# Where the split activations of a two-block transformer kernel begin in SBUF

## The chip, the core and the metric

The kernel runs on one core of a Trainium2 chip. TensorE (PE) multiplies, VectorE (DVE) and ScalarE (ACT) do the element-wise work, GpSimd (POOL) does a few memsets, SyncE (SP) issues the transfers of the weights. The metric is the device time of one execution in microseconds; the time before is the median of three executions.

## What is computed

Two transformer blocks, one after the other, on one sequence of 256 tokens by 1024 features in float32. The first mixes stick-breaking attention with a recurrence (RWKV-7) and ends in a gated feed-forward; the second mixes dilated attention with a gated convolution, attends to a memory of 256 rows, and ends in a squared-ReLU feed-forward. Cut to the products with weights:

```python
# first block
proj = rms_norm(x) @ w_in                       # 1024 -> 5376
merged = gates0 * (o_sb @ w_sb_out) + gates1 * (o_rw @ w_rw_out)
x = x + rms_norm(merged @ w_o)
f = (silu(h @ w_ffn_gate) * (h @ w_ffn_up)) @ w_ffn_down   # 1024 -> 2816 -> 1024
x = x + rms_norm(f)
# second block
x = x + concat(rms_norm(attn), rms_norm(conv)) @ w_out     # from h @ w_in_2, 1024 -> 3072
x = x + softmax(q k^T / 16) v @ w_o_mem                    # q from h, k and v from mem
x = x + relu(h @ w_up)**2 @ w_down                         # 1024 -> 4096 -> 1024
return rms_norm(x)
```

## The kernel before

**How a product with weights is made.** Every float32 operand is split into a rounded high part and the rest: an activation `x` into `xh` and `xl`, a weight slab into `whi` and `wlo`. Three matmuls replace one: `xh·whi`, `xl·whi`, `xh·wlo`. Weights come in slabs of 512 KB (128 partitions of 4 KB each), a `wraw` buffer of three in turn; `slab` (L171) issues the transfer on SP's queue, casts to `whi` on ACT (L182) and subtracts to `wlo` on DVE (L183). A slab holds 4 row blocks of 256 columns, so it feeds 4 x 2 x 3 = **24 matmuls** in `block` (L247): for each half of the columns and each row block the three products above.

**Which operand moves.** In the usual case a 128 x 128 piece of `whi` or `wlo` is loaded into the array (the stationary operand, 512 bytes in each partition) and 256 columns of an activation, 1024 bytes in each partition, are streamed against it (the moving operand). In a name of the profile such as `mm<-xh,whi` the moving operand stands first. With `tok=True` (`w_sb` columns for v, the v columns of `w_in_2` and of `w_kv_mem_2`) the roles are swapped: `mm<-whi,xh`. The last product, `w_down_2` in `tokens`, is swapped too, with slabs of 512 columns: 512 columns of `whi` or `wlo` move against 128 tokens of `ah` or `al`, in 384 matmuls at L262.

**The activations.** `gh, gl` (unnormed input of the first three groups of `w_rw`), `xh, xl` (140 slabs: most of both blocks), `sh, sl` and `oh, ol` (outputs of attention and recurrence), `zh, zl` with the upper half of `xh, xl` (`w_o`), `fh, fl` (22 slabs' worth of `w_ffn_down`), `memh, meml` (8 slabs for k, 8 for v), `yh, yl` (`w_out_2`, 8 slabs), `xoh, xol` (`w_o_mem_2`, 8 slabs), `ah, al` (`w_down_2`).

**What sets the places in SBUF.** Tiles are laid out by pools that stack up in the order in which they are opened, each tile at the next multiple of 32 bytes. The pools of the weights, `wraw`, `whi`, `wlo`, begin at a multiple of 1024 in each partition, so a stationary piece of a slab begins 0 or 512 bytes behind a multiple of 1024. An activation begins where the tiles under it happen to end: `cst`, `vec` and small tiles of 8, 16 or 32 bytes among them. Each row block of an activation is 1024 bytes long, so all row blocks of one begin equally far behind a multiple of 1024.

## Time and profile before

| | |
|---|---|
| median of three executions | 851.95 us (851.76 to 854.29) |
| the profiled execution | 853.44 us, of which its span 851.7 us |
| granted TensorE clock, mean over the span | 0.994 of 2.4 GHz |
| PE busy | 829.5 us, 97% of the span, 6508 matmuls |
| DVE, ACT, POOL busy | 565.3, 464.9, 5.4 us |
| mean rate of the transfers | 168 GB/s, DMA engines busy 30 to 80% of each slice |

Matmuls overlap in the pipeline: a matmul of 256 columns is listed as 280 ns long, while the next one starts some 118 ns after it. How fast TensorE goes is therefore read from the distance between the starts of matmuls, not from their length.

### The profile page before, as it was taken

Reading aid. Unit: us, or ns where it says so; the run is one execution under the profiler, and the core shown is the slowest. Engines: PE = TensorE matmul, PEld = TensorE weight load, DVE = VectorE, ACT = ScalarE, POOL = GpSimd, SP = SyncE. Lnnn points to the kernel's source line nnn. Section 1 sums busy time; section 2 is a strip of 40 time slices with the busy share of each in tenths; the row PEclk is TensorE's granted clock in tenths of the full one; section 3 lists DMA queues with packets and bytes.
Section 4 is the critical chain, followed back from the end, with each engine's and each line's share of the span. In section 5 each row is a group of like instructions: output and inputs, shape, how many; then the busy total and the mean of one; then the engine's idle time right before and its main releaser. Section 6 shows DMA issues by size and latency. Waiting matters only on the chain.

```text
span 851.7 us, 15759 instructions
## 1 busy us (share of the span) xinstructions
PE 829.5 (97%) x6508; PEld 788.4 (93%) x6508; DVE 565.3 (66%) x790; ACT 464.9 (55%) x714; POOL 5.4 (1%) x14
## 2 busy tenths in 40 slices
PE   5999998999999999999999999999999999999996
PEld 5798987999999999999999998999999999988884
DVE  6858689455888776666545876689576666654543
ACT  6497355643577654445445657457455565553432
POOL 0001001000000000000000000000000000000000
PEclk9999999999999999999999999999999999999999
DMA  8434443542464765555555564455524555556551
GB/s 283 149 133 159 136 130 117 160 140 87 145 251 144 225 189 183 195 177 197 173 187 186 158 202 149 148 174 184 188 95 153 176 172 177 193 178 193 179 193 50
DMA packets 44631, 142.88 MB, mean 168 GB/s; under 512 B 8976, under 2 KB 9744, under 8 KB 44304
## 3 DMA queue, kind: packets, MB, share of 16 engines
q1 hardware_dynamic: 43840, 139.25, 50.7%
q10 hardware_dynamic: 720, 2.63, 0.8%
q8 instruction: 51, 0.84, 0.4%
q14 instruction: 20, 0.16, 0.1%
HBM read 139.17 MB, written 2.69 MB: 167 GB/s over the span
## 4 chain that ended last, share of the span: by engine, by line
PE 90%; DVE 5%; DMA 2%; ACT 2%; issue 1%; SPq 0%; ACTq 0%; DVEq 0%
PE mm L247 68%; PE mm L262 11%; DMA wraw<-in_w_rw 2%; PE pz L262 2%; DVE wlo L183 1%; PE po L262 1%; ACT whi L182 1%; PE px L262 1%; PE mgnh L262 1%; PE nv L262 1%; DVE prw L736 1%; PE kv L247 1%; PE ssum L262 1%; DVE pr L718 1%; DVE TF L719 0%
## 5 line engine op out<-in xcount | busy, mean ns | idle before, releaser
L183 DVE TENSOR_TENSOR wlo<-wraw,whi 128x1024 fp32r<-128x1024 f32 x254 | 308.2, 1215 | 198.8 <-ACT whi L182 197.3
L182 ACT CAST whi<-wraw 128x1024 fp32r<-128x1024 f32 x254 | 264.8, 1044 | 291.5 <-PE mm L247 174.9
L247 PE MATMUL mm<-xh,whi 128*128 128x256 f32 x1120 | 319.3, 285 | 0.0
L247 PE MATMUL mm<-xh,wlo 128*128 128x256 f32 x1120 | 316.1, 282 | 1.8 <-DVE wlo L183 1.8
L247 PE MATMUL mm<-xl,whi 128*128 128x256 f32 x1120 | 316.1, 282 | 0.0
L247 PEld LDWEIGHTS mm<-xh,whi 128*128 128x128 f32 x1120 | 212.0, 189 | 3.8 <-issue 2.2
L247 PEld LDWEIGHTS mm<-xh,wlo 128*128 128x128 f32 x1120 | 211.8, 189 | 2.9 <-DVE wlo L183 2.2
L247 PEld LDWEIGHTS mm<-xl,whi 128*128 128x128 f32 x1120 | 211.8, 189 | 0.9 <-issue 0.7
L262 PE MATMUL mm<-whi,ah 128*128 128x512 f32 x128 | 50.6, 395 | 0.0
L262 PE MATMUL mm<-whi,al 128*128 128x512 f32 x128 | 50.6, 395 | 0.0
L262 PE MATMUL mm<-wlo,ah 128*128 128x512 f32 x128 | 50.6, 395 | 0.0
L247 PE MATMUL mm<-fh,whi 128*128 128x256 f32 x176 | 49.1, 279 | 0.0
L247 PE MATMUL mm<-fl,whi 128*128 128x256 f32 x176 | 49.1, 279 | 0.0
L247 PE MATMUL mm<-fh,wlo 128*128 128x256 f32 x176 | 49.1, 279 | 0.0
L247 PEld LDWEIGHTS mm<-fl,whi 128*128 128x128 f32 x176 | 33.1, 188 | 0.0
L247 PEld LDWEIGHTS mm<-fh,wlo 128*128 128x128 f32 x176 | 33.1, 188 | 0.0
L247 PEld LDWEIGHTS mm<-fh,whi 128*128 128x128 f32 x176 | 33.1, 188 | 0.0
L262 PEld LDWEIGHTS mm<-whi,al 128*128 128x128 f32 x128 | 24.1, 188 | 5.8
L262 PEld LDWEIGHTS mm<-wlo,ah 128*128 128x128 f32 x128 | 24.1, 188 | 5.8
L262 PEld LDWEIGHTS mm<-whi,ah 128*128 128x128 f32 x128 | 24.1, 188 | 5.7
L247 PE MATMUL rw<-gh,whi 128*128 128x256 f32 x48 | 14.2, 296 | 9.0 <-ACT whi L182 9.0
L247 PE MATMUL mm<-memh,whi 128*128 128x256 f32 x64 | 18.8, 294 | 0.0
(349 smaller groups left out, 1379.9 us busy)
## 6 DMA issues: line engine op xcount, KB each, us to landing
wraw<-in_w_up SPq DMA_DIRECT2D x32, 512.0 KB, 3.5
wraw<-in_w_down SPq DMA_DIRECT2D x32, 512.0 KB, 4.3
wraw<-in_w_in SPq DMA_DIRECT2D x24, 512.0 KB, 4.2
wraw<-in_w_ffn_gate SPq DMA_DIRECT2D x22, 512.0 KB, 3.8
wraw<-in_w_ffn_up SPq DMA_DIRECT2D x22, 512.0 KB, 3.3
wraw<-in_w_ffn_down SPq DMA_DIRECT2D x20, 512.0 KB, 3.5
wraw<-in_w_gate SPq DMA_DIRECT2D x16, 512.0 KB, 3.3
wraw<-in_w_kv_mem SPq DMA_DIRECT2D x16, 512.0 KB, 3.3
```

The costliest lines, as they stand in the source:

```text
L182: nc.scalar.copy(hi[:, :w], raw[:, :w])
L183: nc.vector.tensor_sub(lo[:, :w], raw[:, :w], hi[:, :w].bitcast(F32))
L247: self.nc.tensor.matmul(ps[:, c, :], lhsT, rhs, start=first, stop=last, skip_group_check=True)
L262: self.nc.tensor.matmul(out, lhsT, rhs, start=start, stop=stop, skip_group_check=True)
L718: nc.vector.tensor_mul(pr[:, :, :, :t + 1], tri[:, :, :, :t + 1], q)
L736: nc.vector.tensor_mul(pr, left[:, r:r + 4, :].rearrange("p r (o i) -> p r o i", o=1).to_broadcast([P, 4, 16, 16]), right.rearrange("p (o ...
```

## The change

Tiles are created in another order, some small ones move into a new tile `small`, and tiles called `shift` are put in as fill. A `shift` tile has one instruction, a memset of one element in each partition on POOL. After it every split activation begins 192 bytes behind a multiple of 1024, and `ah, al` 832 bytes behind one. The weights' pools move too, but still begin at a multiple of 1024. `oh, ol` of the recurrence come from the ring of tag `s4` and no longer from that of tag `rv`. The small tiles `st`, `st2` and `rt` move to other pools.

Bytes behind a multiple of 1024 at which the operands begin, in the two built programs, and the same for the **distance** (begin of the moving operand minus begin of the stationary one, taken modulo 512, since the two halves of a slab's columns are 512 bytes apart):

| activation | before | after | distance before | distance after |
|---|---|---|---|---|
| `xh, xl`, `zh, zl` moving | 480 | 192 | 480 | 192 |
| `gh, gl` | 800 | 192 | 288 | 192 |
| `sh, sl` | 800 | 192 | 288 | 192 |
| `oh` / `ol` | 672 / 544 | 192 | 160 / 32 | 192 |
| `memh, meml` moving | 256 | 192 | 256 | 192 |
| `fh, fl` | 288 | 192 | 288 | 192 |
| `yh, yl` | 320 | 192 | 320 | 192 |
| `xoh, xol` | 352 | 192 | 352 | 192 |
| `xh, xl` stationary | 480, 992 | 192, 704 | 32 | 320 |
| `memh, meml` stationary | 256, 768 | 192, 704 | 256 | 320 |
| `ah, al` stationary | 320, 832 | 832, 320 | 192 | 192 |

(The token halves of a stationary activation lie 512 bytes apart, so there are two begins.)

The core of the diff:

```diff
+PHASE = 192
@@ class Net
         self.keep = pool("keep")
+        self.cst = self.keep.tile([P, NRES], F32, name="cst")
+        self.vec = self.keep.tile([P, NVEC], F32, name="vec")
+        self.small = self.keep.tile([P, 8], F32, name="small")
+        self.ones = self.keep.tile([P, P], F32, name="ones")
         self.pr = pool("wraw", 3)
         self.ph = pool("whi", 4)
         self.pl = pool("wlo", 4)
-        self.cst = self.keep.tile([P, NRES], F32, name="cst")
-        self.vec = self.keep.tile([P, NVEC], F32, name="vec")
-        self.xh = self.keep.tile([P, KC, T], F32R, name="xh")
...
+        acts = pool("acts")
+        self.shift(acts, PHASE)
+        self.xh = acts.tile([P, KC, T], F32R, name="xh")
+        self.xl = acts.tile([P, KC, T], F32R, name="xl")
+        self.zh = acts.tile([P, NP, T], F32R, name="zh")
+        self.zl = acts.tile([P, NP, T], F32R, name="zl")
+
+    def shift(self, pool, bytes_):
+        t = pool.tile([P, bytes_ // 4], F32, name="shift")
+        self.nc.gpsimd.memset(t[:, 0:1], 0.0)
@@ first
         one = ctx.enter_context(tc.tile_pool(name="one", bufs=1))
+        n.shift(one, 608)
         s4 = ctx.enter_context(tc.tile_pool(name="s4", bufs=14))
         dr = ctx.enter_context(tc.tile_pool(name="dr", bufs=1, space=DRAM))
+        n.shift(ctx.enter_context(tc.tile_pool(name="gap", bufs=1)), 640)
...
-            oh, ol = norm["o"] = [s4.tile([P, NP, T], F32R, tag="rv", name=k, bufs=3) for k in ("oh", "ol")]
+            oh, ol = norm["o"] = [s4.tile([P, NP, T], F32R, tag="s4", name=k) for k in ("oh", "ol")]
@@ memory
-    rt = n.rstd_tok(mem, [acc], D)
+    rt = n.rstd_tok(mem, [acc], D, out=n.small[:, 4:6])
@@ hybrid
         pool = ctx.enter_context(tc.tile_pool(name="hyb", bufs=1, reuse_waits="tile"))
+        yh = pool.tile([P, KC, T], F32R, name="yh")
+        yl = pool.tile([P, KC, T], F32R, name="yl")
...
-            st = tmp.tile([P, 2, 8], F32, tag="st2", name="st2", bufs=2)
+            st = pool.tile([P, 2, 8], F32, tag="st2", name="st2", bufs=2)
@@ cross
         pool = ctx.enter_context(tc.tile_pool(name="xat", bufs=1, reuse_waits="tile"))
+        oh = pool.tile([P, KC, T], F32R, name="xoh")
+        ol = pool.tile([P, KC, T], F32R, name="xol")
...
-            st = tmp.tile([P, 8], F32, tag="st", name="st", bufs=4)
+            st = pool.tile([P, 8], F32, tag="st", name="st", bufs=4)
@@ mlp
         pool = ctx.enter_context(tc.tile_pool(name="mlp", bufs=1, reuse_waits="tile"))
+        n.shift(pool, 832 - PHASE)
+        ah = pool.tile([P, 32, T], F32R, name="ah")
+        al = pool.tile([P, 32, T], F32R, name="al")
```

No engine but POOL gets, loses or reorders an instruction. POOL's row before, from the first memset of the recurrence (`TF` its block-diagonal factor, `SA` its states, `TT` its transposed inverse) to its end:

```order
L709 MEMSET TF 128x544 [waits DVE_49,Activation_49]
L713 MEMSET TF 64x8 [waits Pool_49]
L713 MEMSET TF 64x8 x3
L842 MEMSET SA_1849 128x1024 [waits DVE_49,Pool_49]
L842 MEMSET SA_1850 128x1024 [waits DVE_49,PE_49]
L842 MEMSET SA_1851 128x512 [waits DMAHW4_49,DMAHW3_49,DVE_49]
L751 MEMSET TT_1319 128x1024 [waits DMAHW6_49,DMAHW5_49,DMAHW7_49,DVE_49,Activation_49]
L751 MEMSET TT_1320 128x1024 [waits DMAHW1_49,DVE_49,PE_49]
```

Three memsets of `shift` now stand ahead of it and one behind it. And this is the same row after:

```order
L121 MEMSET shift 128x1 x3
L720 MEMSET TF 128x544 [waits DVE_49,Activation_49]
L724 MEMSET TF 64x8 [waits Pool_49]
L724 MEMSET TF 64x8 x3
L853 MEMSET SA_1861 128x1024 [waits DVE_49,Pool_49]
L853 MEMSET SA_1862 128x1024 [waits DVE_49,PE_49]
L853 MEMSET SA_1863 128x512 [waits DMAHW4_49,DMAHW3_49,DVE_49]
L762 MEMSET TT_1331 128x1024 [waits DMAHW6_49,DMAHW5_49,DMAHW7_49,DVE_49,Activation_49]
L762 MEMSET TT_1332 128x1024 [waits DMAHW1_49,DVE_49,PE_49]
L121 MEMSET shift 128x1 [waits DVE_49,PE_49]
```

The last `shift` waits for readers of the tiles that lay in its place. On ACT one cast of `oh`, at the end of the recurrence, has other waits. Before:

```order
L145 ACTIVATE lgv<-lgv 128x512 [waits Activation_49]
L266 CAST oh<-yc 128x512 [waits DVE_49]
L182 CAST whi<-wraw 128x1024 [waits DMAHW4_49,PE_49]
L266 CAST oh<-yc 128x512 [waits DVE_49]
L182 CAST whi<-wraw 128x1024 [waits DMAHW5_49,PE_49]
```

After, on the same engine and at the same place:

```order
L156 ACTIVATE lgv<-lgv 128x512 [waits Activation_49]
L277 CAST oh<-yc 128x512 [waits DMAHW4_49,DVE_49,Pool_49]
L193 CAST whi<-wraw 128x1024 [waits DMAHW4_49,PE_49]
L277 CAST oh<-yc 128x512 [waits DVE_49]
L193 CAST whi<-wraw 128x1024 [waits DMAHW5_49,PE_49]
```

`oh` lies where `TT` lay, so its first cast also waits for `TT`'s memset and transfer.

## Rows read from the trace of the kernel before

**Rows 1.** Busy us, share of the span and number of instructions, from the page.

```profile
PE 829.5 (97%) x6508; PEld 788.4 (93%) x6508; DVE 565.3 (66%) x790; ACT 464.9 (55%) x714; POOL 5.4 (1%) x14
```

**Rows 2.** Waits of PE: us in total, times, longest.

```profile
PE rw L247 <- ACT whi L182: 9.0, 1, 9.0
```

**Rows 3.** The chain that ended last: by line, then pieces (start us, us, what).

```profile
by line: PE mm L247 68.5%; PE mm L262 10.7%; DMA wraw<-in_w_rw 2.0%; PE pz L262 1.7%; DVE wlo L183 1.3%; PE po L262 0.9%; ACT whi L182 0.8%; PE px L262 0.8%; issue 0.8%; PE mgnh L262 0.7%; PE nv L262 0.7%; DVE prw L736 0.7%; PE kv L247 0.7%
...
16.06 5.93 DMA wraw<-in_w_rw
...
126.66 1.90 DVE prw L736
...
291.79 175.21 PE mm L247 x1488
```

**Rows 4.** Timeline of PE, `xh` moving: start us, us, what; rows 24 matmuls apart.

```profile
300.15 0.28 PE L247 MATMUL mm<-xh,whi 128*128 128x256 f32 x1
...
302.99 0.28 PE L247 MATMUL mm<-xh,whi 128*128 128x256 f32 x1
```

**Rows 5.** Timeline of PE, 24 apart: `sh` moving.

```profile
220.85 0.28 PE L247 MATMUL mm<-sl,whi 128*128 128x256 f32 x1
...
223.65 0.28 PE L247 MATMUL mm<-sl,whi 128*128 128x256 f32 x1
```

**Rows 6.** Timeline of PE, 24 apart: `xh` stationary, then `ah` stationary (512 columns).

```profile
505.22 0.28 PE L247 MATMUL mm<-whi,xh 128*128 128x256 f32 x1
...
508.03 0.28 PE L247 MATMUL mm<-whi,xh 128*128 128x256 f32 x1
...
800.05 0.40 PE L262 MATMUL mm<-wlo,ah 128*128 128x512 f32 x1
...
805.65 0.40 PE L262 MATMUL mm<-wlo,ah 128*128 128x512 f32 x1
```

**Rows 7.** Timeline of PE, 24 apart: `memh` moving, `memh` stationary, `xoh` moving.

```profile
264.57 0.28 PE L247 MATMUL mm<-meml,whi 128*128 128x256 f32 x1
...
267.45 0.28 PE L247 MATMUL mm<-meml,whi 128*128 128x256 f32 x1
...
274.91 0.28 PE L247 MATMUL mm<-whi,meml 128*128 128x256 f32 x1
...
277.79 0.28 PE L247 MATMUL mm<-whi,meml 128*128 128x256 f32 x1
...
646.43 0.28 PE L247 MATMUL mm<-xol,whi 128*128 128x256 f32 x1
...
649.31 0.28 PE L247 MATMUL mm<-xol,whi 128*128 128x256 f32 x1
```

**Rows 8.** Timeline of PE, 24 apart: `yh` moving, then `gh` moving.

```profile
578.89 0.28 PE L247 MATMUL mm<-yl,whi 128*128 128x256 f32 x1
...
581.72 0.28 PE L247 MATMUL mm<-yl,whi 128*128 128x256 f32 x1
...
17.93 0.28 PE L247 MATMUL rw<-gl,whi 128*128 128x256 f32 x1
...
20.76 0.28 PE L247 MATMUL rw<-gl,whi 128*128 128x256 f32 x1
```

**Rows 9.** PE by stretch (us): length, busy (matmuls), granted clock, DMA share, GB/s.

```profile
300.00:400.00 100.00, 100.00 (x847) 1.00 0.56 185
405.50:466.50 61.00, 61.00 (x526) 1.00 0.59 183
263.50:274.00 10.50, 10.50 (x90) 1.00 0.26 92
```

**Rows 10.** Timeline of POOL: its last memset, and what it waited for.

```profile
143.51 0.96 POOL L751 MEMSET TT<- 128x1024 f32 x1 [0.50 <-DMA wraw<-in_w_gate]
```

**Rows 11.** Costliest groups, from the page: busy us, mean ns, idle before, its releaser.

```profile
L183 DVE TENSOR_TENSOR wlo<-wraw,whi 128x1024 fp32r<-128x1024 f32 x254 | 308.2, 1215 | 198.8 <-ACT whi L182 197.3
L182 ACT CAST whi<-wraw 128x1024 fp32r<-128x1024 f32 x254 | 264.8, 1044 | 291.5 <-PE mm L247 174.9
```

More of the change, by code (lines that the diff above doesn't have):

```diff
@@ L104, in __init__ @@
         self.pl = pool("wlo", 4)
-        self.cst = self.keep.tile([P, NRES], F32, name="cst")
-        self.vec = self.keep.tile([P, NVEC], F32, name="vec")
-        self.xh = self.keep.tile([P, KC, T], F32R, name="xh")
-        self.xl = self.keep.tile([P, KC, T], F32R, name="xl")
-        self.zh = self.keep.tile([P, NP, T], F32R, name="zh")
-        self.zl = self.keep.tile([P, NP, T], F32R, name="zl")
+        acts = pool("acts")
[7 more added lines that the diff above has]
+        self.nc.gpsimd.memset(t[:, 0:1], 0.0)
     def psum(self, ctx, **bufs):
@@ L293, in rstd_sum, with rstd_tok @@
         return r
-    def rstd_tok(self, pool, parts, width, square=None):
+    def rstd_tok(self, pool, parts, width, square=None, out=None):
         pr = self.ax("rtok")
@@ L301, in rstd_tok @@
                         start=i == 0 and t == 0)
-        rt = pool.tile([P, 2], F32, name="rt")
+        rt = pool.tile([P, 2], F32, name="rt") if out is None else out
         self.act(rt, pr[:, 0:2], AF.Ln, bias=self.eps, scale=1.0 / width)
@@ L366, in network @@
     n = Net(ctx, tc, io)
-    keep = n.keep
-    eps = keep.tile([P, 4], F32, name="eps")
+    eps = n.small
     nc.vector.memset(eps[:, 0:1], EPS)
@@ L372, in network @@
     nc.vector.memset(eps[:, 3:4], 10.0 * math.log(2.0))
-    n.ones = keep.tile([P, P], F32, name="ones")
     nc.vector.memset(n.ones, 1.0)
@@ L1117, in hybrid @@
         ws, wts = {}, {}
-        yh = pool.tile([P, KC, T], F32R, name="yh")
-        yl = pool.tile([P, KC, T], F32R, name="yl")
         half = [slice(64 * r_, 64 * r_ + 64) for r_ in range(2)]
@@ L1213, in cross @@
         nc.vector.tensor_scalar(rn, rt, -1.0, None, op0=ALU.mult)
-        oh = pool.tile([P, KC, T], F32R, name="xoh")
-        ol = pool.tile([P, KC, T], F32R, name="xol")
         qh, ql, ws, wts = {}, {}, {}, {}
@@ L1320, in mlp @@
         banks = n.together([("w_up_2", g) for g in range(4)], n.xh, n.xl, norm)
-        ah = pool.tile([P, 32, T], F32R, name="ah")
-        al = pool.tile([P, 32, T], F32R, name="al")
         n.weave(turned())
```

## The prediction

> **What bounds the kernel now.** I read the busy times first: PE 97%, DVE 66%, ACT 55%, POOL 1% [rows 1]. As a busy PE is no proof of a bound, the waits of PE came next: the longest is 9.0 us, once, at the start, where the first slabs come in [rows 2]. The chain that ended last says the same: the products with weights (L247 and L262) are most of it; DMA and DVE stand on it only at the start and in the recurrence (the pieces at 16 and at 126 us), and from 291.79 us on one piece holds 1488 matmuls [rows 3]. So from about 211 us on the end is set by the distance between the starts of matmuls. Ahead of that PE is also full for long stretches, but DVE and ACT have a share of the chain.
>
> That distance is the thing to look at. Rows 24 matmuls (one slab) apart give it to half a nanosecond, as 0.01 us over 24 is 0.4 ns:
>
> - `xh` moving: 302.99 - 300.15 = 2.84 us, 118.3 ns each [rows 4]; over 100 us, (100 + 0.28)/847 = 118.4 [rows 9].
> - `sh` moving: 2.80 us, 116.7 ns [rows 5]; `fh` moving, over 61 us: 61.28/526 = 116.5 ns, 2.80 us too [rows 9].
> - `xh` stationary: 2.81 us, 117.1 ns; `ah` stationary, 512 columns: 5.60 us, 233.3 ns, which is 2 x 116.7 [rows 6].
> - `memh` moving, `memh` stationary, `xoh` moving: 2.88 us, 120.0 ns [rows 7].
> - `yh` and `gh` moving: 2.83 us, 117.9 ns [rows 8].
>
> The same instruction on the same shape, at the same granted clock of 1.00, the level of 2.4 GHz [rows 9], takes 116.7 to 120.0 ns. What differs is where the operands begin. By distance (moving minus stationary, modulo 512; the table of the change): 288 gives 2.80 and, with `gh`, 2.83; 320 gives 2.83; 480 gives 2.84; 256 and 352 give 2.88; 32 (`xh` stationary) gives 2.81; 192 (`ah`) gives 2.80 for each 256 columns. It is not the moving begin alone: with `xh` and with `memh` stationary the weights move from the same begins and take 2.81 and 2.88 [rows 6, 7]. It isn't the transfers either: the stretch with `memh` has the slower matmuls and half the traffic, 92 GB/s against 183 with `fh` [rows 9]. I call 2.80 us a slab the floor, because three distances and both lengths meet there and no row lies under it.
>
> **The change part by part.** No instruction of PE, DVE, ACT or SP is added, taken away or reordered; what is to be priced is the distance of 192.
>
> *The price of a slab at 192.* The one row with this distance is `ah`, at the floor, but its matmuls are twice as long [rows 6]. The nearest of 256 columns are `yh` at 320 and `gh` at 288, both 2.83, and `sh` and `fh` at 288, at 2.80 [rows 5, 8, 9]. Modulo 128 the slowest, 256 and 352, fall on 0 and 96, the fast ones on 32 and 64, and 192 falls on 64. Ends: 2.80 (nothing in the trace is lower; I allow a little below it for the range) and 2.88 [rows 7]. I take 2.80, by the row that has the distance itself.
>
> *The sum, in slabs of 24 matmuls, before minus after:*
>
> - `xh, xl` moving, 140 slabs: 140 x 0.04 = 5.6 us [rows 4, 5]. 768 of these 3360 matmuls, 32 slabs, start before 211 us, where DVE or a DMA is partly on the chain [rows 3]. I count half of their 1.28 us, so 5.6 - 0.64 = 4.96.
> - `zh, zl`, 4 slabs with the begin of `xh`: 0.16.
> - `memh` moving and `xoh` moving, 8 slabs each: 16 x 0.08 = 1.28 [rows 7].
> - `yh`, 8 slabs, 8 x 0.03 = 0.24, and `gh`, 6 slabs, 0.18 [rows 8].
> - `fh`, 22 slabs, `sh`, 4, and the 384 matmuls with `ah`: at the floor already, 0. `ah`'s two begins only trade places.
> - `memh` stationary, 8 slabs: its distance becomes 320, which is `yh`'s before, so 2.88 - 2.83: 0.40 [rows 7, 8]. `xh` stationary, 8 slabs, goes to 320 too: 2.81 to 2.83, a loss of 0.16 [rows 6, 8].
> - `oh`, 4 slabs with two begins in turn: left at 0; its ends are -0.16 and +0.32 by the rows above.
>
> 4.96 + 0.16 + 1.28 + 0.24 + 0.18 + 0.40 - 0.16 = **7.1 us**.
>
> *The rest at nothing.* The four memsets of one element stand on POOL, which is busy 5.4 us in all [rows 1]; three run at the start, and the last comes behind all other POOL work, where only the kernel's end stands behind it; the readers that it waits for are done in the memory attention. The first cast of `oh` now waits for the memset and the transfer of `TT`; the memset ends at 144.5 us [rows 10], and the recurrence multiplies with `TT` long before `oh` exists, so this wait has run out when ACT gets to it. If it had not, the casts of slabs queued behind it on ACT would be late, and PE with them. The products with two float32 operands (scores, recurrence) get other begins too, some better, some worse. By the chain's lines they are some 5% of it [rows 3]; I have no row that sorts them by begin and put them at 0, with half a microsecond either way in the range. DVE and ACT read and write at other begins; no row prices that. They wait for PE in the dense part, so a few ns on each would be covered.
>
> If TensorE runs 1.4% faster there, each slab is wanted in 2.80 us. DVE's part of a slab is 1.22 us and ACT's 1.04, both idle for long before it [rows 11], and the transfers ran at 183 GB/s beside `fh`, which already took 2.80 [rows 9]. So nothing new becomes late.
>
> **The rivals.**
>
> *It lands at 2.83 or 2.84 instead.* `sh` and `gh` have one begin, 800, and differ [rows 5, 8], so the distance alone doesn't settle it: the pattern in which the starts lock in can come out in more than one way. At 2.83: `xh` gains 1.4, `memh` moving and `xoh` 0.8, `memh` stationary 0.4, `zh` 0.04, while `fh` loses 22 x 0.03 = 0.66, `sh` 0.12 and `xh` stationary 0.16: 1.7 us faster, 850.2.
>
> *Nothing changes*, because the begins are not what sorts the rows, or because 192 costs what 480 does: gains and losses within 0.5 us, 852.0. Against it stands that `memh` and `xh` differ both as moving and as stationary operands [rows 4, 6, 7].
>
> The Trainium skill, "SBUF — State Buffer", section "Who interferes with whom", has it so: TensorE has two independent read ports and never waits on anyone, so where two of its operands lie would be all the same. The trace doesn't agree: 116.7 against 120.0 ns for one shape at one clock [rows 5, 7].
>
> The Trainium skill's "TensorE: Matmul & The Clock Gate", section "Back-to-back issue gap", gives N / 2.4 + 2.5 ns for a matmul by itself, 109.2 at 256 columns. If 192 were free of whatever holds the starts apart, the 140 slabs alone would gain 30 us by that estimate; `ah` at 233.3 ns has the distance and does not come near its 215.8 [rows 6].
>
> *Slower: 192 is a slow distance for 256 columns*, as 256 and 352 are, 64 bytes to one side and 160 to the other, and `ah` hides it, since a piece of 512 bytes is then loaded once in 512 moving columns and not in 256. At 2.88 [rows 7]: `xh` loses 140 x 0.04 = 5.6, `fh` 22 x 0.08 = 1.76, `sh` 0.32, `gh` 0.3, `yh` 0.4, `zh` 0.16, `xh` stationary 0.16; `memh` stationary gains 0.4: 8.3 us slower, 860.3. It turns to a loss as soon as a slab with `xh` takes more than 2.84 us.
>
> **How the numbers follow.** The profiled execution took 853.44 us with its span of 851.7; its distances are the kernel's, so 7.1 off it gives 846.3. Against the median of 851.95, which is what is predicted, it is **844.8 us**. Chances: floor 0.58; below the floor, by the same again as the step from `xh` to `fh`, some 839 us, 0.05; 2.83 or near it 0.14; nothing 0.14; slow distance 0.09. The range takes the first, the third and the fourth: from 841 (full gain in the early part, 0.64, and at `oh`, 0.32, the half microsecond of the float32 products, and 0.01 us a slab below the floor on some 200 slabs, 2) to 853 (nothing, with that half microsecond and what `oh` may lose). A difference of 0.3%, 2.6 us, is about what a measurement of this kernel can tell from no change. Faster by more than that, under 849.4: 0.58 + 0.05 + a fifth of the third case = 0.66; within: 0.25; slower: 0.09.
>
> **What would show it right or wrong.** In the profile after, rows of `xh` 24 apart: 2.80 us if right, 2.83 to 2.84 in the second and third cases, 2.88 in the slower one. All moving activations should then take one value, `fh` and `sh` keep 2.80, `ah` keep 5.60, and `xh` and `memh` stationary come together. The waits of PE should stay as they are. Wrong would be: the matmuls gain as said and PE waits more for `whi`, `wlo` or the transfers; or equal distances with different values, which would leave the begins as no cause.

## The result, and the profile after

The changed kernel takes **845.62 us** (median of four executions, 845.12 to 846.25) against 851.86 us of the kernel before beside it; the ratio is 0.9919, with a 95% interval of 0.9907 to 0.993. That is 6.2 us less, and faster by more than 0.3%. The profiled execution took 845.12 us, of which its span 843.4 us, 8.3 us less than the span of before (851.7); part of these 8.3 us is the granted clock, as shown below, so the medians' 6.2 is the better measure of the change.

What bounds the kernel has not changed. From the page of the kernel after, busy us, share of the span and instructions, as [rows 1]; and the longest waits of PE (us in total, times, longest), as [rows 2], first the two behind [rows 2]'s line in the kernel before, then those of the kernel after:

```profile
PE 818.9 (97%) x6508; PEld 777.1 (92%) x6508; DVE 565.0 (67%) x790; ACT 464.5 (55%) x714; POOL 5.7 (1%) x18
```

```profile
PE pz L262 <- DVE zm L784: 2.9, 2, 2.7
PE mm L247 <- DVE wlo L183: 1.8, 1, 1.8
```

```profile
PE rw L258 <- ACT whi L193: 8.6, 1, 8.6
PE pz L273 <- DVE zm L795: 3.1, 2, 2.9
PE mm L258 <- DVE wlo L194: 2.5, 3, 1.3
PE ssum L273 <- DVE sqa L341: 0.8, 1, 0.8
```

(The block product is now at L258, the other matmuls at L273, the cast and the subtraction of a slab at L193 and L194.) The number of PE instructions is the same, and POOL has the four fills. PE is busy 10.6 us less (829.5 and 818.9), but the rest of the span, in which it is idle, has grown from 22.2 to 24.5 us: it waits somewhat longer for DVE (`wlo` 1.8 to 2.5 us, and 0.8 for `sqa` that wasn't among its waits before). So the time was gained in the matmuls, and some 2 us of that gain went into waiting.

But not evenly. Three pieces of the chain that ended last in the kernel after (start us, us, what), the first of which answers to the last line of [rows 3]:

```profile
288.81 175.25 PE mm L258 x1488
...
694.44 51.70 PE mm L258 x456
746.14 88.21 PE mm L273 x378
```

The second and third of them in the kernel before:

```profile
700.51 53.97 PE mm L247 x456
754.48 88.21 PE mm L262 x378
```

The longest piece, 1488 matmuls with `xh` and `fh` moving, took 175.21 us before and takes 175.25 after: no gain at all where I had forecast some 1.6 us from its 40 slabs of `xh`. The piece of 456 with `xh` moving, the same instruction at the same begins, went from 53.97 to 51.70 us, 2.27 us less and three times what I had forecast for its 19 slabs (0.76). The last product is unchanged, as forecast.

The timeline of PE in the kernel after shows why (start us, us, what; the rows of each pair stand 24 matmuls apart, as in [rows 4] to [rows 8]). `xh` moving at 320 us and at 710 us:

```profile
319.74 0.28 PE L258 MATMUL mm<-xh,whi 128*128 128x256 f32 x1
...
322.57 0.28 PE L258 MATMUL mm<-xh,whi 128*128 128x256 f32 x1
...
709.83 0.28 PE L258 MATMUL mm<-xh,wlo 128*128 128x256 f32 x1
...
712.55 0.28 PE L258 MATMUL mm<-xh,wlo 128*128 128x256 f32 x1
```

The first slab takes 2.83 us, the second 2.72: 117.9 and 113.3 ns for each matmul. `fh` moving, then `memh` moving, then `memh` stationary:

```profile
429.75 0.28 PE L258 MATMUL mm<-fl,whi 128*128 128x256 f32 x1
...
432.57 0.28 PE L258 MATMUL mm<-fl,whi 128*128 128x256 f32 x1
```

```profile
261.83 0.28 PE L258 MATMUL mm<-memh,wlo 128*128 128x256 f32 x1
...
264.55 0.28 PE L258 MATMUL mm<-memh,wlo 128*128 128x256 f32 x1
...
271.73 0.28 PE L258 MATMUL mm<-whi,meml 128*128 128x256 f32 x1
...
274.56 0.28 PE L258 MATMUL mm<-whi,meml 128*128 128x256 f32 x1
```

`fh` 2.82 (2.80 before), `memh` moving 2.72 (2.88), `memh` stationary 2.83 (2.88). So at one and the same distance, 192, a stretch of matmuls (a row of them with the same activation, without a pause) takes **one of two spacings, 113.3 or 117.8 ns**: after its first few matmuls it keeps the one it has until it is interrupted. Stretches of more than 40 with a moving activation hold 1313 starts at some 113.3 ns and 2808 at some 117.8; nothing lies between but the first few matmuls of a stretch. 2.80 us, the price I had put on every slab, is taken by none of them.

The mean distance of starts in unbroken rows of matmuls, worked out from all starts in the two traces, in ns:

| | slabs | before | after | gain by slabs x 24 x difference, us |
|---|---|---|---|---|
| `xh` moving | 140 | 118.32 | 116.07 | 7.6 |
| `memh` moving | 8 | 119.78 | 113.82 | 1.1 |
| `xoh` moving | 8 | 119.97 | 116.72 | 0.6 |
| `memh` stationary | 8 | 119.75 | 115.55 | 0.8 |
| `oh` moving | 4 | 118.45 | 113.50 | 0.5 |
| `sh` moving | 4 | 116.76 | 114.69 | 0.2 |
| `zh` moving | 4 | 118.32 | 117.56 | 0.1 |
| `yh`, `gh` moving | 14 | 117.80, 117.53 | 117.76, 117.63 | 0.0 |
| `xh` stationary | 8 | 116.73 | 117.77 | -0.2 |
| `fh` moving | 22 | 116.69 | 117.78 | -0.6 |
| `ah` stationary, 512 columns | 16 | 233.32 | 233.31 | 0.0 |

10.1 us, of which the span shows 8.3 and the medians 6.2. By the chain's pieces, the kernel after was 291.79 - 288.81 = 3.0 us ahead when the long piece began, and gained 5.3 us from there on.

These 3.0 us are not the operands' alone, since the two profiled executions differ in TensorE's clock. In the one of before the granted clock stood at 0.50, the level of 1.2 GHz, from 33.4 to 36.8 us and from 139.2 to 142.6 us; shortly before, TensorE had been idle for 1.76 us and for 2.67 us, waiting for DVE. In the one of after it stayed at 1.00, the level of 2.4 GHz, from 15 us to behind the last matmul. What that is worth shows in one piece of 31 matmuls on the chain, before and then after:

```profile
33.27 5.45 PE mm L247 x31
```

```profile
33.60 3.79 PE mm L258 x31
```

1.66 us of the 3.0 stand in this piece alone, and the second stretch at 0.50 comes on top. What the places themselves gained ahead of the long piece these two executions don't tell. The ratio doesn't hang on it: the four executions of the changed kernel, at mean clocks of 0.993 to 0.997, agree to 1.1 us, and those of the kernel before beside the experiments had 0.994 to 0.998.

### The profile page after: what moved, and what is told of

Same layout as the page of the kernel before. It is cut to its first block, busy times and chain, and to the rows that moved or that the text cites. A ratio compares the mean times of both kernels' runs of the same rounds, so it can differ in the third digit from the quotient of the medians.

```text
span 843.4 us, 15763 instructions
## 1 busy us (share of the span) xinstructions
PE 818.9 (97%) x6508; PEld 777.1 (92%) x6508; DVE 565.0 (67%) x790; ACT 464.5 (55%) x714; POOL 5.7 (1%) x18
## 4 chain that ended last, share of the span: by engine, by line
PE 81%; DVE 9%; ACT 4%; DMA 3%; issue 2%; DVEq 0%; ACTq 0%; SPq 0%
PE mm L258 59%; PE mm L273 11%; DVE wlo L194 3%; PE pz L273 2%; ACT whi L193 1%; DMA mraw<-in_mem 1%; PE rw L258 1%; PE po L273 1%; PE px L273 1%; PE mgnh L273 1%; PE ssum L273 1%; PE nv L273 1%; DVE prw L747 1%; PE kv L258 1%; DVE xl L326 1%
## 5 line engine op out<-in xcount | busy, mean ns | idle before, releaser
L194 DVE TENSOR_TENSOR wlo<-wraw,whi 128x1024 fp32r<-128x1024 f32 x254 | 308.2, 1215 | 191.0 <-ACT whi L193 190.2
L193 ACT CAST whi<-wraw 128x1024 fp32r<-128x1024 f32 x254 | 264.6, 1044 | 282.8 <-PE mm L258 162.5
L258 PE MATMUL mm<-xh,whi 128*128 128x256 f32 x1120 | 316.5, 283 | 0.0
L258 PE MATMUL mm<-xh,wlo 128*128 128x256 f32 x1120 | 313.4, 280 | 1.9 <-DVE wlo L194 1.9
L258 PE MATMUL mm<-xl,whi 128*128 128x256 f32 x1120 | 313.4, 280 | 0.0
L258 PEld LDWEIGHTS mm<-xh,wlo 128*128 128x128 f32 x1120 | 212.1, 189 | 3.2 <-DVE wlo L194 2.9
L258 PEld LDWEIGHTS mm<-xh,whi 128*128 128x128 f32 x1120 | 210.9, 188 | 3.7 <-issue 2.1
L258 PEld LDWEIGHTS mm<-xl,whi 128*128 128x128 f32 x1120 | 210.7, 188 | 0.9 <-issue 0.6
L273 PE MATMUL mm<-wlo,ah 128*128 128x512 f32 x128 | 50.6, 395 | 0.0
L273 PE MATMUL mm<-whi,al 128*128 128x512 f32 x128 | 50.6, 395 | 0.0
L273 PE MATMUL mm<-whi,ah 128*128 128x512 f32 x128 | 50.6, 395 | 0.0
L258 PE MATMUL mm<-fh,whi 128*128 128x256 f32 x176 | 49.5, 281 | 0.0
L258 PE MATMUL mm<-fl,whi 128*128 128x256 f32 x176 | 49.5, 281 | 0.0
L258 PE MATMUL mm<-fh,wlo 128*128 128x256 f32 x176 | 49.5, 281 | 0.0
L258 PEld LDWEIGHTS mm<-fh,wlo 128*128 128x128 f32 x176 | 33.8, 192 | 0.0
L258 PEld LDWEIGHTS mm<-fh,whi 128*128 128x128 f32 x176 | 33.0, 188 | 0.0
L258 PEld LDWEIGHTS mm<-fl,whi 128*128 128x128 f32 x176 | 33.0, 188 | 0.0
L273 PEld LDWEIGHTS mm<-whi,al 128*128 128x128 f32 x128 | 24.1, 188 | 5.8
L273 PEld LDWEIGHTS mm<-wlo,ah 128*128 128x128 f32 x128 | 24.1, 188 | 5.8
L273 PEld LDWEIGHTS mm<-whi,ah 128*128 128x128 f32 x128 | 24.1, 188 | 5.7
L258 PE MATMUL rw<-gh,whi 128*128 128x256 f32 x48 | 14.9, 310 | 8.6 <-ACT whi L193 8.6
L258 PE MATMUL mm<-memh,whi 128*128 128x256 f32 x64 | 18.5, 288 | 0.0
```

The lines of the kernel that those rows point to most:

```text
L193: nc.scalar.copy(hi[:, :w], raw[:, :w])
L194: nc.vector.tensor_sub(lo[:, :w], raw[:, :w], hi[:, :w].bitcast(F32))
L258: self.nc.tensor.matmul(ps[:, c, :], lhsT, rhs, start=first, stop=last, skip_group_check=True)
L273: self.nc.tensor.matmul(out, lhsT, rhs, start=start, stop=stop, skip_group_check=True)
```

## The experiments

Each run was made beside runs of the kernel before, which took 849.9 to 852.1 us (medians) on these chips. Streams, the changed kernel once more and the run with all distances at 256 were executed once, the others four times. The code of streams is given in outline. "Distance" is as before, moving begin minus stationary begin. Names like `xh` in a stream stand for operands of that role.

**The distance by itself.** A kernel with nothing but streams of matmuls, in the order in which `block` issues them, at sixteen distances, each entered two or three times; then with the stationary operands begun 96 bytes further on; then with 512 moving columns. No transfer and no cast runs beside them.

```python
for d in range(0, 512, 32):            # a<d>: whi, wlo at 0, xh and xl at d
    for entry in range(3): stream(w0, w1, x0 + d, x1 + d)
for d in (192, 256, 288, 480):         # b<d>: the same distance, everything 96 on
    for entry in range(3): stream(v0 + 96, v1 + 96, x0 + d + 96, x1 + d + 96)
for d in range(0, 512, 64):            # c<d>: 512 columns of a slab move
    for entry in range(2): wide(...)
```

> A kernel of its own, not the reference's computation: streams of 72 matmuls of 256 columns in the kernel's order (three products, 4 row blocks, 2 halves) with nothing else running, for the 16 distances 0, 32, ..., 480 of the moving behind the stationary operand, each restarted three times after a pause of different length; then four distances with the stationary operand begun 96 bytes further on; then 512 columns of weights against a stationary activation at 8 distances. Theory (the distance sets the spacing): 192 gives 113.3 or 117.8 ns as in the changed kernel, 256 and 352 give 120.0, 288 gives 116.7 or 117.8, 320 117.8, 480 118.3, and the shifted pairs the same values as their unshifted ones; 512 columns give 233.3 at 192. Rival (the begins of single operands count, or the traffic of the other engines does): the shifted pairs differ from the unshifted by 1 ns or more, or all distances give one value.

Streams of 72 matmuls of 256 columns, and of 48 of 512 (timeline of PE: start of the first, us to the end of the last, what, count, idle time ahead):

```profile
201.51 8.43 PE L68 MATMUL a192x<-x,w 128*128 128x256 f32 x72 [0.60 <-ACT res L44]
...
257.67 8.89 PE L68 MATMUL a256x<-x,w 128*128 128x256 f32 x72 [0.60 <-ACT res L44]
267.02 8.66 PE L68 MATMUL a288x<-x,w 128*128 128x256 f32 x72 [0.46 <-ACT res L44]
...
426.12 8.43 PE L68 MATMUL a448x<-x,w 128*128 128x256 f32 x72 [0.60 <-ACT res L44]
...
472.34 8.74 PE L68 MATMUL b192x<-x,v 128*128 128x256 f32 x72 [0.73 <-ACT res L50]
481.69 8.44 PE L68 MATMUL b192x<-x,v 128*128 128x256 f32 x72 [0.60 <-ACT res L50]
490.59 8.89 PE L68 MATMUL b256x<-x,v 128*128 128x256 f32 x72 [0.46 <-ACT res L50]
...
574.99 11.20 PE L79 MATMUL c0x<-w,x 128*128 128x512 f32 x48 [0.46 <-ACT res L50]
...
658.96 11.46 PE L79 MATMUL c192x<-w,x 128*128 128x512 f32 x48 [0.73 <-ACT res L55]
```

Four things are to be seen. The time goes by the distance and not by the single begins, since `b192` and `b256`, 96 bytes further on, give what `a192` and `a256` give. It repeats after 256 bytes, not 512: `a448` is `a192`, and all of 256 to 480 gave what 0 to 224 gave. The order of the distances is not the same at 512 columns: 192 is the fastest for 256 columns and the slowest of the four tried for 512, where 0 is the fastest. And `b192`, entered three times, took 8.74 us once and 8.44 the other time shown: the two spacings are there without any other work on the chip.

In the later half of each stream, and beside it what the kernel before had at that distance modulo 256 (ns):

| distance modulo 256 | streams alone | in the kernel before |
|---|---|---|
| 0 | 120.0 | `memh` moving 119.8, `memh` stationary 119.75 |
| 32 | 116.7 | `fh` 116.7, `sh` 116.8, `xh` stationary 116.7, but `gh` 117.5 |
| 64 | 117.8 | `yh` 117.8 |
| 96 | 120.0 | `xoh` 120.0 |
| 128 | 118.5 to 118.8 | |
| 160 | 117.3 to 118.7 | |
| 192 | 113.3 (117.8 once in nine entries) | |
| 224 | 118.3 | `xh` 118.3, `zh` 118.3 |
| 0 / 64 / 192, 512 columns | 226.7 / 228.8 / 233.3 | `ah`, at 192, 233.3 |

Except for `gh` every row of the kernel before with one distance is what that distance gives (`oh`, at 160 and 32 in turn, had 118.5).

**The changed kernel once more,** without an edit.

> The changed kernel once more. In its profile stretches of matmuls at one and the same distance of 192 run at 113.3 ns or at 117.8 ns each. Theory one, the spacing a stretch locks into is settled by how it starts, and that is the same in every execution: the same stretches run at the same spacing, total 845.1 to 846.3. Rival, it is settled by chance in each execution: stretches swap between 113.3 and 117.8, and the total moves by up to 4 us for the longest of them (959 matmuls x 4.4 ns).

846.78 us, half a microsecond over the range expected. The long piece of the chain, and `gh` moving, 24 apart, in this execution:

```profile
291.50 175.25 PE mm L258 x1488
```

```profile
19.75 0.28 PE L258 MATMUL rw<-gh,wlo 128*128 128x256 f32 x1
...
22.46 0.28 PE L258 MATMUL rw<-gh,wlo 128*128 128x256 f32 x1
```

The long piece is slow again to the hundredth, but `gh` took the faster spacing (2.71 us, where the first profile has 117.8 ns in the same stretch), as did `zh`, and one stretch with `memh` took the slower. So the spacing isn't a property of an operand. Some stretches fall the same way in each execution, others don't.

**All distances at 256 (that is, 0).** The constant alone:

```diff
-PHASE = 192
+PHASE = 256
```

> The changed kernel with 256 bytes in place of 192 for all moving activations, ah and al as in the changed kernel. If the distance is the cause, xh, fh, yh, xoh and memh moving all take 120.0 ns: against the changed kernel 3360 x 3.9 ns for xh (116.1 on average there) and 528 x 2.2 for fh, 192 x 2.2 for yh, 192 x 3.3 for xoh and 192 x 6.2 for memh, together some 17 us, so about 862. Rival, that the change gains by something else (fill, pools, other engines): 845 to 847.

858.7 us beside 849.9, 3 us under the 862 expected. The same piece of the chain:

```profile
290.96 178.54 PE mm L258 x1488
```

178.54 us for 1488 matmuls is 120.0 ns each, where the streams had 120.0. The pools' new order, the fills and the moved small tiles are all still there; only the begins differ from the changed kernel, and every stretch with a moving activation took what the streams take at distance 0 (119.8 to 120.0 ns). So the distance is the cause, and the slower side that I had feared exists, at another place than the one chosen.

**The last product at 192 and not 832.**

```diff
-        n.shift(pool, 832 - PHASE)
         ah = pool.tile([P, 32, T], F32R, name="ah")
```

> The changed kernel without the fill in the last feed-forward, so that ah and al begin 192 bytes behind a multiple of 1024 and the weights move at a distance of 320 from them. If the distance counts for the last product as for the others, 320 is 117.8 ns for 256 columns against 116.7, so about 235.6 instead of 233.3 ns: 384 x 2.2 = 0.85 us slower than the changed kernel. Rival, that the last product does not care: 233.3 ns, the same time.

842.83 us (ratio to before 0.9912, interval 0.9896 to 0.9929). `ah` stationary, 24 matmuls apart:

```profile
789.77 0.39 PE L273 MATMUL mm<-wlo,ah 128*128 128x512 f32 x1
...
795.26 0.39 PE L273 MATMUL mm<-wlo,ah 128*128 128x512 f32 x1
```

5.49 us, where `ah` at 832 took 5.60 as in [rows 6]: 228.8 ns. I had expected a loss and was wrong. The part of the change that gives the last product a place of its own, 832, puts it at distance 192, the worst one for 512 columns; leaving it out is 384 x 4.4 ns = 1.7 us better in these rows. The ratio of the whole, 0.9912, can't be told from the 0.9919 of the changed kernel.

**How narrow it is.** The streams again, at steps of 4 bytes around 192 and of 8 or 16 at 512 columns.

```diff
-DISTS = list(range(0, 512, 32))
+DISTS = (168, 176, 180, 184, 188, 196, 200, 204, 208, 212, 216, 220)
+WIDE = (8, 16, 24, 32, 48, 208, 224, 232, 240, 248)
```

> Streams alone again, not the reference's computation: distances from 168 to 220 in steps of 4 and 8 bytes, four restarts each, 72 matmuls of 256 columns; and 512 columns of weights against a stationary activation at 8, 16, 24, 32, 48, 208, 224, 232, 240, 248. In the first study the distance counted modulo 256, 192 locked at 113.3 ns or at 117.8 ns, and 512 columns took 226.7 ns at 0 and 233.3 at 192. If the spacing is settled in steps of 32 bytes, all distances from 192 to 220 are like 192 and those from 168 to 188 like 160 (117.3 to 118.8). If the distance counts continuously, the 113.3 ns lie in the middle of a window around 192 and some neighbour locks at it in every restart. Rival: the two spacings at 192 have nothing to do with the distance, and each neighbour shows both.

```profile
173.43 8.74 PE L60 MATMUL a188x<-x,w 128*128 128x256 f32 x72 [0.73 <-ACT res L42]
...
210.86 9.02 PE L60 MATMUL a196x<-x,w 128*128 128x256 f32 x72 [0.73 <-ACT res L42]
```

4 bytes to either side of 192 the faster spacing is gone: 188 gives 117.8 to 118.9 ns, 196 gives 121.7 to 122.2, which is slower than any distance that is a multiple of 32. No other distance of the twelve gave 113.3. At 512 columns 8 bytes off 0 already gives 233.4 (and 16 gives 228.3).

**The three products have three distances.** `block` issues `xh·whi`, `xl·whi`, `xh·wlo` in turn; the change puts `xh` and `xl` at 192, and `whi` and `wlo` both at 0. Streams with `xh` at h, `xl` at l, `wlo` at w times 64 bytes, all 64 combinations, each entered four times: behind the stream before it, once more, behind one float32 matmul of 256 columns, and behind four of 128.

```python
for h in range(4):
    for l in range(4):
        for w in range(4):
            for entry in range(4):     # h<h>l<l>w<w>
                between(entry); stream(w0, w1 + 64 * w, x0 + 64 * h, x1 + 64 * l)
```

> Streams alone, not the reference's computation: 48 matmuls of 256 columns in the kernel's order, for all 64 choices of the begins of xh (h), xl (l) and wlo (w) in steps of 64 bytes, whi at 0, each entered in four ways (directly, after a pause, after one float32 matmul of 256 columns, after four of 128 columns and a pause). The open question is what settles whether a stretch at 192 runs at 113.3 or at 117.8 ns. If the entry alone settles it, h3 l3 w0 (all distances 192) shows both and no other choice is free of a slow entry. If the sequence of distances settles it, some choice of begins locks at 113.3 in all four entries, and others never do; h1 l1 w0 should stay at 117.8 and h0 l0 w0 at 120.0 as in the first study.

The third and fourth entry (48 matmuls each) of the changed kernel's placing, `h3l3w0`, and of the same with `wlo` at 128, `h3l3w2`:

```profile
1459.59 6.00 PE L67 MATMUL h3l3w0x<-x,w 128*128 128x256 f32 x48
...
1466.24 5.70 PE L67 MATMUL h3l3w0x<-x,w 128*128 128x256 f32 x48
...
1506.94 5.81 PE L67 MATMUL h3l3w2x<-x,w 128*128 128x256 f32 x48
...
1513.40 5.71 PE L67 MATMUL h3l3w2x<-x,w 128*128 128x256 f32 x48
```

Behind the matmul of 256 columns `h3l3w0` takes 6.00 us and stays at 117.8 ns; behind those of 128, 5.70 and 113.3. `h3l3w2` needs a few matmuls longer in its third entry (5.81) and then runs at 113.3 in all four. It is the only one of the 64 that did so; the slowest took 121.1 to 121.5.

**`wlo` at 128 in the whole kernel.**

```diff
+LOW = 128
         self.ph = pool("whi", 4)
+        self.shift(pool("turn"), LOW)
         self.pl = pool("wlo", 4)
         acts = pool("acts")
-        self.shift(acts, PHASE)
+        self.shift(acts, PHASE - LOW)
```

> The changed kernel with wlo begun 128 bytes behind a multiple of 1024 and everything else in its place (a fill of 128 bytes goes in ahead of the wlo pool, and the one ahead of xh shrinks from 192 to 64). If the two spacings of the changed kernel, 113.3 and 117.8 ns, are a matter of how a stream enters, and the placing whi 0, wlo 128, activations 192 always enters the faster one, every stretch with a moving activation runs at 113.3: xh gains 3257 x 2.7 ns = 8.9 us, fh 527 x 4.4 ns = 2.3, yh 0.8, xoh 0.6, gh, zh, sh and memh 1.2 together, some 14 us in all, 831.5 +- 2.5 us (the products with stationary xh, memh and ah get a mixed distance, unpriced). If the slower spacing comes from something else in the kernel (the transfers or the casts running beside it, which the streams alone don't have), it stays near 845; fh, slow in every run so far, is the place to look.

834.2 us, ratio to before 0.979 (0.9761 to 0.982), 2.7 us over the 831.5 expected. The same piece of the chain (one of its 1488 records is not in it):

```profile
290.59 168.56 PE mm L260 x1487
```

168.56 us where it was 175.25: every stretch with a moving activation now runs at 113.3 ns, with `fh` at 113.33 and the mean of `xh`, its entries included, at 113.74. Of the products left unpriced, `memh` stationary went from 115.6 to 117.7 ns. The transfers and casts beside it are the same. So the slower spacing in the changed kernel was not theirs.

**What stands ahead of a stretch.** The changed kernel with all its places, but the sum of squares ahead of the long piece made by two matmuls of 128 columns and not by one of 256:

```diff
-            self.mm(ps[:, :T], self.ones, p, start=i == 0)
+            for c in range(0, T, by):
+                self.mm(ps[:, c:c + by], self.ones, p[:, c:c + by], start=i == 0 and c == 0)
...
-            pair(n.rstd_sum(tmp, [n.squares(tmp, pairs(n.x))], D, "rs"))))
+            pair(n.rstd_sum(tmp, [n.squares(tmp, pairs(n.x))], D, "rs", by=P))))
```

> The changed kernel with one difference in what stands ahead of its longest dense piece, 1488 matmuls with xh and fh moving, which began at 288.8 us and took 175.25 us at 117.78 ns in every run so far with whi and wlo both at 0: the sum of squares there (ssum) is made by two float32 matmuls of 128 columns and not by one of 256. All places in SBUF stay. If the spacing is settled by how a stream enters, this piece can change to 113.33 ns: 1488 x 4.45 = 6.6 us less, 168.6 us for the piece and about 839 us in all (in the streams alone, whi and wlo at 0 and activations at 192 took 117.8 behind one float32 matmul of 256 columns and 113.3 behind those of 128). If something else holds it at the slower one, the transfers or casts beside it or the length of the piece, it stays at 175.2 us and the total at 845.6.

838.59 us (ratio to before 0.9864, 0.9823 to 0.9905). What stands ahead of the piece in the kernel after, and then in this one (timeline of PE, which lists a float32 matmul twice):

```profile
288.22 0.59 PE L273 MATMUL ssum<-sqa,ones 128*128 128x256 f32 x2
```

```profile
287.56 0.60 PE L273 MATMUL ssum<-sqa,ones 128*128 128x128 f32 x4
```

And the piece itself, in this one's chain:

```profile
288.17 168.66 PE mm L258 x1488
```

168.66 us, as expected to the tenth. The same places, the same 1488 matmuls, another matmul ahead of them, 6.6 us. (The order of some matmuls in the recurrence, ahead of 250 us, also moved with this edit, and some short stretches fell the other way; the piece itself doesn't depend on those, since in the four other profiled executions with these places it took 175.25 whatever had happened ahead; in the changed kernel once more the matmuls right ahead of `ssum` even ran at 113.3 ns.) That what stands ahead of a stretch can settle its spacing is shown for this piece, in one profiled execution. Whether the faster one comes each time isn't: of the four executions of this run one took 843.88 us, 4 to 7 us more than the other three (836.7 to 839.73), at a mean granted clock of 0.996, no lower than theirs. What in the first few matmuls settles the spacing isn't shown either.

**The last product, and both together.** First streams with the roles of the last product and of the k, v products, `xh` at h, `xl` at l, `wlo` at w times 64 bytes, now with the weights moving:

```python
for wide in (True, False):             # t: 512 columns, s: 256
    for w in (0, 2):
        for h in range(4):
            for l in range(4): stream(x0 + 64 * h, x1 + 64 * l, w0, w1 + 64 * w)
```

> Streams of fp32r matmuls alone, with the roles of the last product and of the k, v products: a stationary 128x128 token piece, xh at h x 64 bytes and xl at l x 64 bytes, against moving weights, whi at 0 and wlo at 0 or 128 (names t for 512 columns, s for 256; then h, l, w). It leaves out the kernel's whole computation. If the three distances of a row block's products count each for itself, then with wlo at 0: t with h0 l0 takes 226.7 ns, h1 l1 233.3, h3 l3 228.8, and s with h1 l1 113.3 (the moving operand then lies 192 behind the stationary one), s with h3 l3 117.8, h0 l0 120.0. With wlo at 128 the stretches h0 l0 should lie between 226.7 and 232 at 512 columns if each product pays for its own distance (about 228.5), and could go either way if the sequence of three counts as one pattern, as it did where activations move.

```profile
281.61 11.35 PE L72 MATMUL th0l0w2x<-w,x 128*128 128x512 f32 x48
...
452.81 11.17 PE L72 MATMUL th2l2w2x<-w,x 128*128 128x512 f32 x48
```

At 512 columns only `h0 l0` with `wlo` at 0 takes 226.7 ns; with `wlo` at 128 the same takes 233.5, and not the mean of its distances. So the sequence counts as one pattern here too. The best with `wlo` at 128 are some 229 (`h2 l2`). At 256 columns `h1 l1 w0`, whose distance is 192 as well, took 113.3 in one entry and 117.8 in three, so at this length 192 is fast with the weights moving too. And `xh` at 64 with `xl` at 192 (`h1 l3 w0`) took 113.3 in all four, a placing that no run tried in the whole kernel.

Then the changed kernel with `ah` at distance 0 (`wlo` at 0):

```diff
-        n.shift(pool, 832 - PHASE)
+        n.shift(pool, 256 - PHASE)
```

> The changed kernel with the last product's ah, al begun 256 bytes behind a multiple of 1024 and not 832 (distance 0 modulo 256, not 192), everything else in its place. If the last product goes by the distance as the streams alone did (226.65 ns at 0, 233.3 at 192), its 384 matmuls take 384 x 6.66 ns = 2.6 us less: 843.1 us. If 228.9 is as fast as it gets beside the transfers, 843.9. If the place doesn't count there, 845.6.

841.2 us (0.9874, 0.9846 to 0.9902). The third piece of the chain, which was 88.21 us:

```profile
744.68 85.71 PE mm L273 x378
```

2.5 us less, 226.7 ns each. The rest of the difference to 845.6, some 2 us and more than I had expected, is not the last product's.

The kernel with `wlo` at 128 and `ah` at distance 128:

```diff
-        n.shift(pool, 832 - PHASE)
+        n.shift(pool, 384 - PHASE)
```

> The kernel with wlo at 128 and, besides, the last product's ah, al begun 384 bytes behind a multiple of 1024 (128 modulo 256). The streams alone gave 229.1 ns for this placing of 512 columns, 231.1 measured in the kernel with wlo at 128 and ah at 832. 384 x 2.0 = 0.8 us less than 834.2: 833.4 us. If the dense stretches lose their lock when the tail changes place, which nothing suggests, more.

831.26 us (0.978, 0.9746 to 0.9813); `ah` went from 231.1 ns, with `wlo` at 128 alone, to 228.9, as the streams had it. And the kernel in which each `wlo` buffer is 128 bytes longer and a slab uses it from the begin that its product wants:

```diff
+        at = (self.turn + (0 if name == "w_down_2" else LOW // 4)) % (2 * LOW // 4)
+        self.turn += LOW // 4
-        lo = self.pl.tile([P, SW], F32R, tag="wlo", name="wlo")
+        lo = self.pl.tile([P, SW + LOW // 4], F32R, tag="wlo", name="wlo")[:, at:at + SW]
...
-        n.shift(pool, 832 - PHASE)
+        n.shift(pool, 256 - PHASE)
```

> Both best placings at once: each wlo buffer gets 128 bytes more, and a slab uses it from the offset that makes it begin at 128 modulo 256, but at 0 for the last product, whose ah, al begin at 0 modulo 256. Stretches with a moving activation keep 113.3 ns as with wlo at 128 everywhere, and the last product goes from 231.1 to 226.7 ns: 384 x 4.4 = 1.7 us less than 834.2, so 832.5 us, 13 us under the changed kernel. If the gains of the two placings overlap in something (a tail that waits for casts or transfers instead), it stays at 834.

```profile
289.68 168.56 PE mm L262 x1487
```

```profile
789.75 0.39 PE L277 MATMUL mm<-whi,ah 128*128 128x512 f32 x1
...
795.19 0.39 PE L277 MATMUL mm<-whi,ah 128*128 128x512 f32 x1
```

**830.46 us** (0.9763, 0.9737 to 0.979), the fastest, by the ratios (0.9763 and 0.9919) some 13 us under the changed kernel: the long piece at 168.56 us and the last product at 5.44 us for 24. The medians of these last two differ by less than their intervals can tell.

## Why the prediction came out right, and where its steps did not

The time, 845.62 us, is 0.8 us from the 844.8 forecast, and the sign is right. By its own steps:

- *What bounds the kernel: the distance between the starts of matmuls.* Right in the main: every experiment that moved only operands' begins moved the spacing of the stretches concerned. But the waits of PE did not stay as they were, which I had named as a sign; PE was idle some 2 us longer than before.
- *The distance sorts the rows, not the moving begin alone and not the transfers.* Right, shown by the shifted streams and by the run with all distances at 256. But I took it modulo 512. It is modulo 256. With that, 288 and 32 are one distance, which explains why `fh` and `xh` stationary had one price in the kernel before; 320 is 64; and the one pair I had left to chance, `gh` and `sh` at one begin with two prices, is the only row that the table doesn't account for.
- *The price of a slab at 192: 2.80 us.* **This is the step that failed.** I took it "by the row that has the distance itself", `ah`, halving a row of 512 columns. The streams show that the two lengths have different orders: 192 is the best distance for 256 columns and among the worst for 512. There was no row in the trace at 192 with 256 columns, so the value was a guess with a row beside it. And "floor" was a wrong word: nothing in the trace being lower showed only that no operand lay at 192. What stands in its place is 2.72 us or 2.83, by the way in which the stretch enters.
- *The sum, 7.1 us.* By the same slabs it would be 10.1; 8.3 came out in the span, part of it by the clock, and 6.2 in the medians. Some 2 us went into PE's idle time; the rest of the difference is not sorted. The total was near because the two spacings, in the shares in which they fell (1313 and 2808 starts), average 116.4 ns, 2.79 us a slab: close to 2.80 by chance. Term by term: `xh` 7.6 and not 5.6, at the faster spacing with 0.12 us a slab, three times the 0.04 forecast, at the slower one with 0.01; `memh` moving and `xoh` 1.8 and not 1.28; `memh` stationary 0.8 and not 0.40 (part of its matmuls, in short rows between others, started 113.4 apart); `oh` and `sh` 0.7 and not 0; `yh` and `gh` nothing and not 0.42, since they fell into the slower spacing; `fh` lost 0.6 that I had at 0; `xh` stationary lost 0.2, as forecast; `ah` nothing, as forecast.
- *Half of the early part counts.* Not decided. The kernel after was 3.0 us ahead when the long piece began, but 1.66 us of that stand in one piece that ran at the lower granted clock before, which the forecast left out, and the prices were wrong themselves.
- *The rest at nothing.* The fills on POOL hid, as forecast. The last memset of `TT`, in the timeline of POOL in the kernel after (start us, us, what, idle time ahead), ends at 143.2 us, and the first cast of `oh` began at 218.7, its first product at 221.9:

```profile
142.24 0.96 POOL L762 MEMSET TT<- 128x1024 f32 x1 [0.50 <-DMA wraw<-in_w_gate]
```

  That nothing else would become late was not quite right: PE waited longer for DVE, by 0.7 us for `wlo` and 0.8 for `sqa`. It did not get worse with faster matmuls: in the fastest kernel `xh` ran at 113.3 ns, 4% under 2.84 us a slab, and PE's idle time was 832.3 - 807.7 = 24.6 us, as in the changed kernel.
- *The rivals.* "The pattern in which the starts lock in can come out in more than one way" was the right mechanism, but I made it a rival to the forecast and priced it as 2.83 for all. It was not one or the other: both spacings stand in one execution, one at 2.83 and one below what I called the floor. "192 is a slow distance, and `ah` hides it" was wrong in sign and right in its reason: that a row of 512 columns says little on 256. (256 and 352 don't stand to either side of 192, as I wrote: both lie above it, and modulo 256 the one is 64 above and the other 96 below.) At 256, the slow distance, the kernel takes 858.7 us, close to the 860.3 that I had worked out for one. "Nothing changes" fell with it.
- From two independent read ports and a TensorE that never waits on anyone (the Trainium skill, "SBUF — State Buffer", "Who interferes with whom") I had drawn, for the rival that nothing changes, that the places of its own two operands would be all the same. That conclusion fails: with nothing else running, two begins 4 bytes apart gave 113.3 and 121.7 ns. Whether the ports are the reason no run shows. The 109.2 ns that the Trainium skill gives for a matmul by itself in "TensorE: Matmul & The Clock Gate", "Back-to-back issue gap", was reached by no run here; the lowest is 113.3, and 226.7 at 512 columns, where its formula has 215.8.

Of what would have shown it wrong I had named "equal distances with different values, which would leave the begins as no cause". Equal distances did show different values (and `xh` and `memh` stationary, at 117.8 and 115.6 ns, didn't come together), and the begins are the cause all the same: a place can decide which spacings are possible, and the entry which of them comes.

## What to carry to other kernels

Where the starts of back-to-back fp32r matmuls are the bound, look at them over one slab to a hundredth of a microsecond, and sort them by where the moving and the stationary operands lie against each other, for each length of the moving side apart; a row at another length is no price. Expect that one placing can have more than one steady spacing, so price a range and look stretch by stretch: a mean over stretches hid here that the longest piece had gained nothing. Compare the granted clock of two profiled executions before a difference of a few us is put down to a change. When only part of the stretches gain, ask for the placing that reaches the faster spacing from each entry (here activations at 192, with the high and low weight parts half a period of 256 bytes apart): it was worth more than the change itself.

## What the runs showed of the hardware that I had not expected

- The spacing of fp32r matmuls with a new stationary operand each depends on the distance of the operands' begins in a partition modulo 256 bytes: 113.3 to 123.3 ns for 256 columns, 226.7 to 233.4 for 512, at a granted clock of 1.00 and with nothing else running. It isn't smooth: 188, 192 and 196 gave 117.8, 113.3 and 121.7 as their lowest.
- The spacing belongs to the sequence, not to a single matmul: the mean of three single distances predicted neither `h3 l3` with `wlo` at 128 (113.3) nor `h0 l0` with `wlo` at 128 at 512 columns (233.5).
- A stretch keeps the spacing that its first few matmuls come to, over 1488 matmuls and 175 us, and what stood ahead of it, a float32 matmul of 256 columns or two of 128, was worth 6.6 us in the profiled executions.
- What makes the spacing, which port or buffer two reads meet in, no run here shows.
